# Hybrid decoder block on one core: when the mixing product's later operands are split, and who makes two SwiGLU chunks' low parts

## The chip, the cores and the metric

The kernel runs on 1 core of one Trainium2 chip. The metric is the device time of one execution in microseconds.

## The reference

One decoder block on 512 tokens of width 1024, all in float32. What matters here is the last steps of the token mixers and the channel mixer behind them:

```python
y_a = u @ conv_w_out + conv_b_out                    # 1024 x 1024
y_b = (hb * gelu(z_rg)) @ lru_w_out                  # 1280 x 1024
m = sigmoid(z_ga) * y_a + sigmoid(z_gb) * y_b
x = x + m @ w_mix_out                                # the mixing product, 1024 x 1024
h = rmsnorm(x, norm2_g)
x = x + (silu(h @ ffn_w1) * (h @ ffn_w3)) @ ffn_w2   # SwiGLU, width 2816
return rmsnorm(x, norm_f_g)
```

Ahead of these stand an input norm, one wide input projection (`w_in`), a 31-tap causal convolution with a layer norm, and a gated linear recurrence with block-diagonal gates.

## The kernel before, in words

**Matmuls in two parts.** TensorE works on the type fp32r. To keep float32 accuracy each operand is split into a high part (a cast to fp32r, made by ScalarE, `split_to`, line 133) and a low part (the operand minus its high part, a subtraction, line 129). A product is then three matmuls: high by high, high by low, low by high. The low part's engine is an argument: VectorE (`vec`) or GpSimd (`pool_e`).

**Weights.** Weights come in chunks of 128 x 1024. The list `chunks` holds them in the order of use. `emit_chunk` loads a chunk into one of 4 raw buffers (`raws`) through the SP queue, casts its high part on ScalarE and subtracts its low part on the engine that the chunk names (`lo`), into one of 5 buffers (`hls`). `weights(key, ahead)` first emits all chunks up to `ahead` (4 as a rule) behind the one asked for. Tiles `hl_mxb` and `hl_mxt` are chunks of `w_mix_out`, `hl_fb` and `hl_ft` those of the SwiGLU weights.

**The mixing product.** `m @ w_mix_out` and the last SwiGLU product are made by the class `Sevenfold`, with seven products of half size where eight would be plain. Inner blocks are numbered k = 0 to 3. `tile` and `pair` make, on VectorE, sums and differences of the quarters of `m` for each k; `ops[k]` holds a pair that is split at once (`u_`, `sp`) and two tiles that are not split yet, `e` and `va`. `run` makes the products:

- The first pass goes over k = 0 to 3 with the operands `u_` and `sp` into three pairs of PSUM banks, r1, r2 and r5. In the last k the two row blocks of r1 and r2 end first, and `plus` (line 1000, its addition at line 940) adds each into `x2`, the residual stream: four additions of 128 x 512 on VectorE.
- `split_late` splits `e` and `va` of one k, into `mxeb` and `mxvb`: two casts on ScalarE and two subtractions on VectorE. It is called after each k of the first pass once k is at least `lag`, and after each k of the second pass until all are split. `lag` is 0 for the mixing product (`m7`) and `LATE_LAG`, 8, for the last product (`o7`).
- The second pass (`second`) goes over k = 0 to 3 with `e` and `va` into banks r7, r1 and r3; r1 goes on accumulating, so it waits for the additions that read it, and r3 takes the banks of r2. Behind the first k of it four additions take r5 into `x2`.
- The last k and the rest (`third`) stand in `mix_end`, with six more additions, the second norm's statistics, the scaled rows `xs` and their transposes `th` (line 579).

`mix_end` also loads weights for sums that GpSimd makes for later products (`piece_sums`, tiles `fws` and `fwso`, lines 129 and 394), and `full` adds high and low parts on GpSimd (line 1078).

**The order of work.** Most engines' instructions are put in order by the framework: of those that are ready in its own planning, the one traced first is issued first. `tc.manual_schedule` keeps the traced order for the engines it names; it is used for the end of the mixing product but not for its two passes. `tc.issue_after(ins)` queues what is traced inside it, on the engine of `ins`, behind `ins`; instructions on other engines are not bound by it.

**The two SwiGLU chunks.** Blocks 1 and 2 of the SwiGLU product (`BEGUN`) begin early. Their first chunks, `fb11_1`, `fb21_1`, `fb11_2`, `fb21_2`, follow the chunks of `w_mix_out` in the list, and the reach ahead emits the first three of them during the second pass of the mixing product. The list is made by these lines:

```python
for k in BEGUN:
    f_both("b11", k)
    f_both("b21", k)
```

Of the kernel before, what the change touches and what calls it, by code (L numbers as in the profile page):

```python
# [52 lines left out]
BEGUN, BEGUN_LATER = (1, 2), (3,)  # L53
# [1 line left out]
SUMS_DENSE, SUMS_OWN, SUMS_EACH = 20, 52, (60, 68)  # L55


F_MIX, OUT_MIX, LATE_LAG = 2, 1, 8
OUT_IN = 1

KEPT = {2: 1, 3: 2, 4: 3, 5: 4, 6: 5, 7: 6, 8: 7, 9: 7, 10: 7}
# [35 lines left out]
def tile_block(ctx, tc, a, out):  # L97
# [19 lines left out]
    def bank(name):  # L117
        return psum.tile([P, T], F32, tag="mm", name=name)

    def bank2(name):  # L120
        return psum2.tile([P, T], F32, tag="cv", name=name)

    vec, act, pe, pool_e = nc.vector, nc.scalar, nc.tensor, nc.gpsimd
# [15 lines left out]
    def split(name, full, eng, p_=None, copy=act.copy):  # L139
        p_ = p_ or pairt(name)  # L140
        return split_to(*p_, full, eng, copy)
# [7 lines left out]
    def wchunk(key, src, kt, cols, where="hl", lo=pool_e, after=None):  # L149
        chunks.append((key, src, kt, cols, where, lo, after))  # L150
# [101 lines left out]
    class Quartered:  # L252
        def __init__(self, name, w, kh, lo, parts=(), step=None):


            self.name, self.w, self.kh = name, w, kh
            self.step = step or 1
            self.tile = lambda k, i: k + kh * i if self.step == 1 else 2 * k + i
            self.parts = {n: [None] * kh for n in parts}

            self.all_sums = [dram.tile([P, 4, T], F32, tag=f"{name}t_{k}", name=f"{name}t_{k}") for k in range(kh)]
            self.sums = {(n, k): self.all_sums[k][:, i, :] for i, n in enumerate(IN_PLACE) if n not in parts for k in range(kh)}
            self.at = {}

            def quarter(n, k):
                if n[0] == "t":
                    return self.sums[n, k]
                i, h = int(n[1]) - 1, int(n[2]) - 1
                return w[:, self.tile(k, i), h * T : (h + 1) * T]

            def chunk(key, of):
                def load(raw_t):
                    for i, q in enumerate(of):
                        nc.sync.dma_start(raw_t[:, i * T : (i + 1) * T], quarter(*q))

                for i, q in enumerate(of):
                    self.at[q] = (f"{name}{key}", i)
                wchunk(f"{name}{key}", load, len(of), T, lo=lo)


            for p_ in (("b11", "t1", "b21"), ("t2", "t3", "b22"), ("t4",)):
                p_ = [n for n in p_ if n not in parts]
                for k in range(kh):
                    if len(p_) % 2 and k % 2 == 0:
                        chunk(f"{p_[-1]}_{k}", [(p_[-1], i) for i in (k, k + 1) if i < kh])
                    if len(p_) > 1:
                        chunk(f"{p_[0]}_{k}", [(n, k) for n in p_[:2]])
# [4 lines left out]
        def get(self, k, *names, ahead=AHEAD):  # L292

            out = []
            for n in names:
                if n in self.parts:
                    out.append(self.parts[n][k])
                    continue
                key, i = self.at[n, k]
                if key not in self.loaded:  # L300
                    self.loaded[key] = weights(key, ahead)
                h, l = self.loaded[key]
                out.append((h[:, i, :], l[:, i, :]))
            return out
# [22 lines left out]
    mixq = Quartered("mx", a["w_mix_out"][0].rearrange("(k p) n -> p k n", p=P), ND // 2, vec, ("t1", "t4"))  # L327
# [7 lines left out]
    def f_quarter(n, k, w_, c0, c1):  # L335

        c, j = 4 * (int(n[1]) - 1), 2 * k + int(n[2]) - 1
        return w_[:, c + c0 : c + c1, j * P : (j + 1) * P]
# [7 lines left out]
    def f_both(n, k, lo=vec):  # L346

        def load(raw_t):
            for i, w_ in enumerate((w1, w3)):
                if n[0] == "b":  # L350
                    src = f_quarter(n, k, w_, 0, 4)
                else:
                    c, e, _ = WHERE[n]
                    src = f_sums[k][:, i, int(c[1]), :].rearrange("p (k n) -> p k n", k=4)[:, :, e * P : (e + 1) * P]
                newest["any"] = nc.sync.dma_start(raw_t[:, i * T : (i + 1) * T].rearrange("p (k n) -> p k n", k=4), src).ins

        wchunk(f"f{n}_{k}", load, 8, P, lo=lo)
# [81 lines left out]
            yield  # L439

    for k in BEGUN:
        f_both("b11", k)
        f_both("b21", k)

    for k in BEGUN:
        f_both("t4", k, vec if k == BEGUN[0] else pool_e)
# [340 lines left out]
    behind = [None, None]  # L787
# [160 lines left out]


    class Sevenfold:  # L950
        def __init__(self, q, lag=0):
            self.lag, self.kept = lag, 0
            self.q, self.uv, self.ops, self.waiting = q, [], [], []
            self.name, self.kh = q.name, q.kh

# [37 lines left out]
        def run(self, sums, begun, end):  # L993

            n, kh, get = self.name, self.kh, self.q.get
            quarter = lambda p_, cs: tuple(v[:, cs] for v in p_)
            plus = lambda t, h, b_: add(sums[t][h], b_, sums[t][h])  # L1000
            late = []

            def split_late():
                k = len(late)
                if k < kh:
                    late.append((split(f"{n}eb{k}", self.ops[k][2], vec), split(f"{n}vb{k}", self.ops[k][3], vec)))

            r1, r2 = ([bank(f"{n}{r}{i}") for i in range(2)] for r in ("r1", "r2"))
            r5 = [bank2(f"{n}r5{i}") for i in range(2)]
            for k in range(kh):  # L1010
                wb21, wb11, wt1 = get(k, "b21", "b11", "t1")
                u_, sp, e, va = self.ops[k]
                todo = [(r1, quarter(u_, LO), wb11), (r2, quarter(u_, HI), wb21), (r5, (sp[:, LO], sp[:, HI]), wt1)]
                ends = k == kh - 1
                order = [(r, i) for i in range(2) for r in (0, 1)] + [(2, 0), (2, 1)] if ends else [(r, i) for r in range(3) for i in range(2)]
                for r, i in order:
                    self.product(todo[r][0], i, *todo[r][1:], k == 0, ends)
                    if ends and r == 1:
                        plus(i, 0, r1[i])
                        plus(i, 0, r2[i])  # L1020
                if k >= self.lag:
                    split_late()
                begun(k)
            r7, r2 = ([bank(f"{n}{r}{i}") for i in range(2)] for r in ("r7", "r3"))

            def second(k, wb22, wt2, wt3):
                e, va = late[k]
                todo = [(r7, quarter(e, HI), wt3), (r1, quarter(va, LO), wt2), (r2, quarter(e, LO), wb22)]
                ends = k == kh - 1
                order = [(r, i) for i in range(2) for r in (1, 2)] + [(0, 0), (0, 1)] if ends else [(r, i) for r in range(3) for i in range(2)]  # L1030
                for r, i in order:
                    self.product(todo[r][0], i, *todo[r][1:], r != 1 and k == 0, ends, r == 1)

            def third(i, ks):
                for k in ks:
                    self.product(r1, i, quarter(late[k][1], HI), *get(k, "t4"), False, k == kh - 1, True)

            for k in range(kh - 1):
                second(k, *get(k, "b22", "t2", "t3"))
                split_late()  # L1040
                if k == 0:
                    for i in range(2):
                        plus(i, 1, r5[i])
                        plus(2 + i, 1, r5[i])

            act.activation(warm, late[-1][1][0][:, :1].bitcast(F32), AF.Sqrt, scale=0.0, bias=eps_t)
            last = get(kh - 1, "b22", "t2", "t3", ahead=AHEAD - 1)
            end(lambda: second(kh - 1, *last), plus, r1, r2, r7, third)

    m7 = Sevenfold(mixq)  # L1050
    for n, j in enumerate(mixq.order()):
        ws = w_tiles(f"co{j}", ND)
        ps = bank(f"ya{j}")
# [410 lines left out]
```

## Time and profile before

| what | value |
|---|---|
| median of 3 runs | 798.24 us (798.44, 798.24, 797.44) |
| span of the profiled execution | 797.3 us |
| TensorE busy | 786.5 us (99%) |
| VectorE busy | 696.8 us (87%) |
| ScalarE busy | 473.2 us (59%) |
| GpSimd busy | 359.9 us (45%) |
| mean granted TensorE clock | 0.997 |

The page gives the profiled execution's span, from its first to its last instruction, and no other time of that execution; the median of the runs is 0.94 us over that span. Engines are named PE (TensorE), PEld (its weight loads), DVE (VectorE), ACT (ScalarE), POOL (GpSimd) and SP (SyncE, which issues most DMAs). A row of a timeline has start and duration in us, engine, line, operation, what is written from what, and in brackets the idle time before it with what ended that. A row of the table of windows has the stretch, its length, the busy time of PE, PEld, DVE, ACT and POOL with the number of instructions, the granted clock, the DMA share and GB/s. A line such as L129 or L940 is that of a helper which many parts use, so the tile names tell the instructions apart.

### The profile page before, as it was taken

Reading aid. Unit: us, or ns where it says so; the run is one execution under the profiler, and the core shown is the slowest. Engines: PE = TensorE matmul, PEld = TensorE weight load, DVE = VectorE, ACT = ScalarE, POOL = GpSimd, SP = SyncE. Lnnn points to the kernel's source line nnn. Section 1 sums busy time; section 2 is a strip of 40 time slices with the busy share of each in tenths; the row PEclk is TensorE's granted clock in tenths of the full one; section 3 lists DMA queues with packets and bytes.
Section 4 is the critical chain, followed back from the end, with each engine's and each line's share of the span. In section 5 each row is a group of like instructions: output and inputs, shape, how many; then the busy total and the mean of one; then the engine's idle time right before and its main releaser. Section 6 shows DMA issues by size and latency. Waiting matters only on the chain.

```text
span 797.3 us, 12582 instructions
## 1 busy us (share of the span) xinstructions
PE 786.5 (99%) x4374; PEld 689.1 (86%) x4374; DVE 696.8 (87%) x1097; ACT 473.2 (59%) x674; POOL 359.9 (45%) x347
## 2 busy tenths in 40 slices
PE   8999999999999999999999999999999999999996
PEld 7988888888888888888887898999999999888885
DVE  5899999999998997985799968898877798999956
ACT  7546688777679654562326467554555555556743
POOL 2576778788779988853360482113312221000000
PEclk9999999999999999999999999999999999999998
DMA  7745566577776786879887887588988898778652
GB/s 216 196 127 175 162 190 195 179 238 229 200 247 202 243 272 212 281 232 296 266 309 238 277 263 230 150 273 264 355 298 289 301 326 294 239 236 258 206 171 105
DMA packets 181074, 188.13 MB, mean 236 GB/s; under 512 B 14119, under 2 KB 142035, under 8 KB 181011
## 3 DMA queue, kind: packets, MB, share of 16 engines
q1 hardware_dynamic: 172195, 156.66, 63.1%
q0 software_dynamic: 8672, 30.41, 11.0%
q8 instruction: 34, 0.56, 0.3%
q10 hardware_dynamic: 144, 0.26, 0.1%
q14 instruction: 29, 0.24, 0.1%
HBM read 145.48 MB, written 38.80 MB: 231 GB/s over the span
## 4 chain that ended last, share of the span: by engine, by line
PE 83%; DVE 9%; DMA 4%; issue 2%; ACT 2%; SPq 0%; DVEq 0%; ACTq 0%
PE z L539 35%; PE fr L1218 24%; PE or L991 13%; PE f L539 3%; PE g L860 3%; PE mxr L991 3%; DMA raw_lo<-in_lru_w_out_dram 1%; DMA raw_co<-in_conv_w_out_dram 1%; DMA mxws<-in_w_mix_out_dram 1%; PE fr L1262 1%; DVE hl_co L129 1%; PE yb L539 1%; DVE hl_mxb L129 1%; DVE mxws L129 1%; DVE sga L1056 1%
## 5 line engine op out<-in xcount | busy, mean ns | idle before, releaser
L733 DVE SCALAR_TENSOR_TENSOR cv<-u,par,cv 128x511 f32<-128x511 f32 (+17 forms) x240 | 162.6, 728 | 1.1 <-ACT cv L730 0.9
L129 POOL TENSOR_TENSOR hl_in<-raw_in,hl_in 128x1024 fp32r<-128x1024 f32 x51 | 123.2, 2422 | 63.6 <-ACT hl_in L133 45.1
L129 POOL TENSOR_TENSOR fws<-fws 128x256 f32<-128x256 f32 x120 | 104.6, 874 | 78.6 <-DMA fws<-in_ffn_w_dram 72.9
L398 POOL DMA_DIRECT2D ot<-fwso x21 | 15.3, 731 | 164.4 <-DVE fwso L129 156.7
L1218 PE MATMUL fr<-hs_0h,hl_ft 128*128 128x256 f32 x320 | 59.2, 283 | 0.0
L133 ACT CAST hl_in<-raw_in 128x1024 fp32r<-128x1024 f32 x51 | 53.2, 1043 | 3.2 <-POOL fws L394 1.3
L129 DVE TENSOR_TENSOR hl_ft<-raw_ft,hl_ft 128x1024 fp32r<-128x1024 f32 x39 | 47.5, 1218 | 5.5 <-ACT hl_ft L133 5.5
L1218 PEld LDWEIGHTS fr<-hs_0h,hl_ft 128*128 128x128 f32 x320 | 50.6, 192 | 0.0
L133 ACT CAST hl_ft<-raw_ft 128x1024 fp32r<-128x1024 f32 x40 | 41.8, 1046 | 13.2 <-PE fr L1218 9.9
L129 DVE TENSOR_TENSOR hl_fb<-raw_fb,hl_fb 128x1024 fp32r<-128x1024 f32 x30 | 36.7, 1222 | 14.6 <-ACT hl_fb L133 13.8
L1218 PE MATMUL fr<-hs_0l,hl_ft 128*128 128x256 f32 x160 | 45.3, 283 | 0.0
L133 ACT CAST hl_fb<-raw_fb 128x1024 fp32r<-128x1024 f32 x30 | 31.5, 1050 | 20.8 <-PE fr L1218 13.3
L539 PE MATMUL z<-h10h,hl_in 128*128 128x512 f32 (+1 forms) x110 | 41.4, 378 | 0.0
L539 PE MATMUL z<-h17h,hl_in 128*128 128x512 f32 (+1 forms) x110 | 41.1, 376 | 0.0
L539 PE MATMUL z<-h11h,hl_in 128*128 128x512 f32 (+1 forms) x110 | 41.1, 376 | 0.0
L539 PE MATMUL z<-h13h,hl_in 128*128 128x512 f32 (+1 forms) x110 | 41.1, 376 | 0.0
L539 PE MATMUL z<-h14h,hl_in 128*128 128x512 f32 (+1 forms) x110 | 41.1, 376 | 0.0
L539 PE MATMUL z<-h15h,hl_in 128*128 128x512 f32 (+1 forms) x110 | 41.1, 376 | 0.0
L539 PE MATMUL z<-h16h,hl_in 128*128 128x512 f32 (+1 forms) x110 | 41.1, 376 | 0.0
L539 PE MATMUL z<-h12h,hl_in 128*128 128x512 f32 (+1 forms) x110 | 41.1, 375 | 0.0
L133 ACT CAST hl_ob<-raw_ob 128x1024 fp32r<-128x1024 f32 (+1 forms) x23 | 23.4, 1016 | 23.4 <-PE or L991 10.5
L394 POOL TENSOR_TENSOR fws<-fws 128x256 f32<-128x256 f32 x40 | 31.6, 792 | 2.8
(962 smaller groups left out, 2640.6 us busy)
## 6 DMA issues: line engine op xcount, KB each, us to landing
raw_in<-in_w_in_dram SPq DMA_DIRECT2D x52, 512.0 KB
fws<-in_ffn_w_dram SPq DMA_DIRECT2D x80, 256.0 KB
raw_ft<-fs SPq DMA_DIRECT2D x34, 512.0 KB
fs<-fws SPq DMA_DIRECT2D x23, 512.0 KB
ot<-fwso POOLq DMA_DIRECT2D x21, 512.0 KB, 6.0
fwso<-in_ffn_w_dram POOLq DMA_DIRECT2D x40, 256.0 KB, 7.1
fs<-fws POOLq DMA_DIRECT2D x17, 512.0 KB, 4.9
raw_ob<-in_ffn_w_dram SPq DMA_DIRECT2D x33, 256.0 KB
```

Source lines behind the costliest of these rows:

```text
L129: return eng.tensor_tensor(out=o, in0=x, in1=y, op=ALU.subtract)
L133: copy(h, full)
L394: eng.tensor_tensor(out=q11, in0=q22, in1=q11, op=ALU.add)
L398: return queue.dma_start(dest, raw.rearrange("p (m n) -> p m n", m=dest.shape[1]))
L539: pe.matmul(ps, l, r, start=i == 0, stop=i == n - 1)
L733: vec.scalar_tensor_tensor(out=acc[c][:, s:], in0=u[c][:, : T - s], scalar=dw(c, s), in1=acc[c][:, s:], op0=ALU.mult, op1=ALU.add)
L860: pe.matmul(ps, l, r, start=k == 0, stop=k == len(mms) - 1)
L991: pe.matmul(banks[i], l_[:, ts], r_, start=start and n == 0, stop=stop and n == 2, skip_group_check=again)
L1056: vec.scalar_tensor_tensor(out=o, in0=ps, scalar=pc("conv_b_out", j), in1=o, op0=ALU.add, op1=ALU.mult)
L1218: pe.matmul(ps[:, HALVES[i]], lw[:, c, :], rx_, start=not (again or i or c or m), stop=bool(i and c == 3 and m == 2), skip_group_check=True,)
L1262: pe.matmul(self.r4[:, HALVES[i]], lw, rx_, start=not (i or c or m), stop=bool(i and c == 3 and m == 2), skip_group_check=True)
```

## The change

Three things change. `MIX_LATE_LAG` is 2, so in the first pass of the mixing product `split_late` is called after k = 2 and after k = 3 instead of after each k; the parts of k = 2 and 3 are traced after the first and the second k of the second pass. A new flag `behind`, set for the mixing product, puts the `split_late` after the last k of the first pass under `tc.issue_after` of the last of the four additions. And the low parts of the chunks `fb11_1` and `fb21_1` are made by GpSimd instead of VectorE.

```diff
-F_MIX, OUT_MIX, LATE_LAG = 2, 1, 8
+F_MIX, OUT_MIX, MIX_LATE_LAG, LATE_LAG = 2, 1, 2, 8
...
     for k in BEGUN:
-        f_both("b11", k)
-        f_both("b21", k)
+        for n in ("b11", "b21"):
+            f_both(n, k, pool_e if k == BEGUN[0] else vec)
...
     class Sevenfold:
-        def __init__(self, q, lag=0):
-            self.lag, self.kept = lag, 0
+        def __init__(self, q, lag=0, behind=False):
+            self.lag, self.kept, self.behind = lag, 0, behind
...
-            late = []
+            late, last_sum = [], None
...
                     if ends and r == 1:
                         plus(i, 0, r1[i])
-                        plus(i, 0, r2[i])
+                        last_sum = plus(i, 0, r2[i]).ins
                 if k >= self.lag:
-                    split_late()
+                    with tc.issue_after(last_sum) if last_sum and self.behind else nullcontext():
+                        split_late()
                 begun(k)
...
-    m7 = Sevenfold(mixq)
+    m7 = Sevenfold(mixq, MIX_LATE_LAG, True)
```

## The prediction

> **What bounds the kernel now.** I read the page first: one engine fills the span.
>
> ```profile
> span 797.3 us, 12582 instructions
> PE 786.5 (99%) x4374; PEld 689.1 (86%) x4374; DVE 696.8 (87%) x1097; ACT 473.2 (59%) x674; POOL 359.9 (45%) x347
> ```
>
> TensorE is busy in all but 10.8 us of 797.3. Next I cut the span into three stretches with the table of windows, leaving out the start (to 12 us) and the tail (from 787 us), which the change does not touch.
>
> ```profile
> 12.00:434.00 422.00, 422.00 (x1955) 353.24 (x1955) 385.25 (x578) 263.44 (x348) 287.87 (x251) 1.00 0.72 220
> 434.00:440.00 6.00, 4.62 (x20) 3.23 (x19) 6.00 (x10) 3.79 (x6) 0.00 (x0) 1.00 1.05 359
> 440.00:787.00 347.00, 346.91 (x2337) 322.05 (x2336) 294.61 (x483) 194.82 (x292) 68.95 (x90) 1.00 0.79 256
> ```
>
> The second number is TensorE's busy time. Between 12 and 787 us it idles 1.38 us in the one stretch 434 to 440 and 0.09 us in all the rest. So this kernel offers one hole, and it is the turn from the first pass to the second of the mixing product. The timeline of TensorE shows the hole, and the blocks behind it give the undisturbed pace.
>
> ```profile
> 434.70 0.61 PE L991 MATMUL mxr<-hl_mxt,mxeb0h 128*128 128x512 f32 x2
> 436.72 0.40 PE L991 MATMUL mxr<-hl_mxt,mxvb0l 128*128 128x512 f32 x1
> 438.50 0.73 PE L991 MATMUL mxr<-hl_mxt,mxvb0h 128*128 128x512 f32 x2 [1.38 <-DVE x L940]
> 440.67 0.62 PE L991 MATMUL mxr<-hl_mxt,mxeb1h 128*128 128x512 f32 x2
> 444.75 0.62 PE L991 MATMUL mxr<-hl_mxt,mxeb2h 128*128 128x512 f32 x2
> 448.83 0.62 PE L991 MATMUL mxr<-hl_mxt,mxvb3h 128*128 128x512 f32 x2
> 449.28 0.39 PE L991 MATMUL mxr<-hl_mxt,mxvb3l 128*128 128x512 f32 x1
> ```
>
> Blocks 1 and 2 of the second pass (18 matmuls each) take 444.75 - 440.67 = 4.08 and 448.83 - 444.75 = 4.08 us, 0.227 a matmul. Block 0 takes 440.67 - 434.70 = 5.97. It loses 1.89 us: the wait named on the 438.50 row and slower restarts around it. The releaser is a VectorE addition at L940, `plus`, which takes a first-pass bank into `x2`; block 0 accumulates on into that bank, so it must wait. VectorE's timeline says why the addition is late.
>
> ```profile
> 434.75 0.69 DVE L129 TENSOR_TENSOR mxeb1l<-mxe,mxeb1h 128x512 fp32r<-128x512 f32 x1
> 435.36 0.68 DVE L940 TENSOR_TENSOR x<-mxr,x 128x512 f32<-128x512 f32 x1
> 435.95 0.68 DVE L129 TENSOR_TENSOR mxvb1l<-mxv,mxvb1h 128x512 fp32r<-128x512 f32 x1
> 436.56 0.68 DVE L940 TENSOR_TENSOR x<-mxr,x 128x512 f32<-128x512 f32 x1
> 437.15 0.68 DVE L129 TENSOR_TENSOR mxeb2l<-mxe,mxeb2h 128x512 fp32r<-128x512 f32 x1
> 437.75 0.68 DVE L940 TENSOR_TENSOR x<-mxr,x 128x512 f32<-128x512 f32 x1
> ```
>
> Additions and low parts alternate, 0.60 us apart. The third addition (bank r1 of row block 1) ends at 437.75 + 0.68 = 438.43, and TensorE restarts at 438.50. The low parts of k = 1 and 2 between them are not needed until 440.67 and 444.75.
>
> **The later parts.** With `MIX_LATE_LAG` 2 the parts of k = 0 are made in the first pass after k = 2, those of k = 1 after k = 3 with their VectorE half queued behind the fourth addition, those of k = 2 and 3 in the second pass. Per k this moves two casts on ScalarE and two subtractions on VectorE, and no DMA. Three low parts leave the places ahead of the third addition (the 434.75, 435.95 and 437.15 rows): 3 x 0.60 = 1.80 us. It then ends at about 436.63. TensorE without the hole wants it three matmuls after 436.06 (six matmuls of 0.227 after 434.70), so at 436.74: the wait and the slow restarts go, 1.89 us, with at most 0.15 left since the two times nearly touch. The operands `x2` were loaded before (no addition waits on a DMA in these rows); an addition 1.8 us earlier could meet such a wait, which no row excludes, and its bound is the hole itself.
>
> What is late next? First the parts that were put back. VectorE does the same list of work, so the list ends no sooner, and the parts of k = 3 come last in it.
>
> ```profile
> 441.29 0.69 DVE L129 TENSOR_TENSOR mxvb3l<-mxv,mxvb3h 128x512 fp32r<-128x512 f32 x1
> 443.09 1.22 DVE L129 TENSOR_TENSOR hl_mxt<-raw_mxt,hl_mxt 128x1024 fp32r<-128x1024 f32 x1
> 444.22 1.28 DVE L940 TENSOR_TENSOR x<-mxr,x 128x512 f32<-128x512 f32 x2
> 445.42 1.22 DVE L129 TENSOR_TENSOR hl_fb<-raw_fb,hl_fb 128x1024 fp32r<-128x1024 f32 x1
> 446.62 1.22 DVE L129 TENSOR_TENSOR hl_fb<-raw_fb,hl_fb 128x1024 fp32r<-128x1024 f32 x1
> 448.75 1.25 DVE L129 TENSOR_TENSOR hl_fb<-raw_fb,hl_fb 128x1024 fp32r<-128x1024 f32 x1 [0.86 <-ACT hl_fb L133]
> 449.93 4.06 DVE L940 TENSOR_TENSOR x<-mxr,x 128x512 f32<-128x512 f32 x6
> ```
>
> The mixing work ends at 444.22 + 1.28 = 445.50. In the changed order the four additions of r5 and the last t2 chunk are traced ahead of the parts of k = 3, so I take these as last: `mxvb3l` ready near 445.5 instead of 441.98. TensorE, 1.89 earlier, wants it at 449.28 - 1.89 = 447.39. Left alone, 1.9 us of slack hides it. The casts cost nothing either, as long as ScalarE keeps the hole that its row shows:
>
> ```profile
> 440.05 1.05 ACT L133 CAST hl_mxt<-raw_mxt 128x1024 fp32r<-128x1024 f32 x1 [2.22 <-DMA raw_mxt<-mxt]
> 442.15 0.19 ACT L555 ACTIVATION_READ_ACCUMULATOR xs<-x 128x1 f32 x1
> 443.58 1.06 ACT L133 CAST hl_fb<-raw_fb 128x1024 fp32r<-128x1024 f32 x1 [1.25 <-PE mxr L991]
> 444.94 1.06 ACT L133 CAST hl_fb<-raw_fb 128x1024 fp32r<-128x1024 f32 x1 [0.30 <-PE mxr L991]
> 447.67 1.06 ACT L133 CAST hl_fb<-raw_fb 128x1024 fp32r<-128x1024 f32 x1 [1.66 <-PE mxr L991]
> ```
>
> The four casts for k = 2 and 3 are half as wide as the 1.06 us cast, an estimate of 2.1 us for all; 2.22 us are free ahead of 440.05. If that cover is gone they push the first `hl_fb` cast by up to 2 us, and nothing needs that chunk before 460.
>
> **The two low parts on GpSimd.** VectorE loses the 445.42 and 446.62 rows, 2 x 1.2 = 2.4 us. GpSimd gains two subtractions of the same form, ahead of work that waits for a DMA:
>
> ```profile
> 448.19 2.42 POOL L129 TENSOR_TENSOR fws<-fws 128x256 f32<-128x256 f32 x2 [31.50 <-DMA fws<-in_ffn_w_dram]
> 457.24 0.74 POOL L1078 TENSOR_TENSOR hf<-h20h,h20l 128x256 f32<-128x256 f32 x1 [1.77 <-DVE h20l L583]
> L129 POOL TENSOR_TENSOR hl_in<-raw_in,hl_in 128x1024 fp32r<-128x1024 f32 x51 | 123.2, 2422 | 63.6 <-ACT hl_in L133 45.1
> 460.26 0.28 PE L1218 MATMUL fr<-h20h,hl_fb 128*128 128x256 f32 x1
> ```
>
> One takes 2.42 us by the group of its form. The casts ahead of them wait on TensorE, so they come 1.89 earlier: the first can start at 441.69, behind the two squares at 442.34, and GpSimd starts at about 442.8 to 443.4 and ends the second at 447.6 to 448.2. The chunk is first used at 460.26 - 1.89 = 458.4, which is 10 us later. The queue behind them, the SwiGLU weights' sums, is held until 448.2 at most, where its DMA lets it begin at 448.19 now; if that DMA comes 1.9 earlier too, the sums lose up to 1.9 us of it and end no later than now, and the 1.77 us that GpSimd idles at 457.24 is cover besides.
>
> The price is elsewhere. Two rows from a much earlier stage show what a VectorE subtraction with both inputs in SBUF does while such a GpSimd subtraction runs:
>
> ```profile
> 171.13 2.40 POOL L129 TENSOR_TENSOR hl_in<-raw_in,hl_in 128x1024 fp32r<-128x1024 f32 x1
> 171.53 2.54 DVE L129 TENSOR_TENSOR xb7l<-xb,xb7h 128x512 fp32r<-128x512 f32 x1
> ```
>
> The VectorE one starts 0.40 after GpSimd's, ends 0.54 after GpSimd's end (174.07 against 173.53), and takes 2.54 instead of 0.69: it stood until GpSimd was done. The additions do not: six at 449.93 take 4.06 us, 0.68 each, while GpSimd makes the sums that begin with the 448.19 row; they read one input from PSUM. The Trainium skill, GPSIMD Engine Reference, section 8 "Key points", says that GpSimd shares its SBUF interfaces with VectorE and contends with VectorE instructions that have two SBUF inputs; these rows agree. The page gives no duration: if contention were only a slowing shared by both engines, the sum below would lie between -1.79 and its own -0.94; by the row, in which VectorE stands still, it is -0.94.
>
> So which VectorE work falls into 443 to 448? The third `hl_fb` (the 448.75 row) stays on VectorE; its cast ends at 447.67 + 1.06 - 1.89 = 446.84. If GpSimd holds until 447.6 or 448.2, it ends 1.2 later at 448.8 to 449.4. Behind it on VectorE are the six additions of the 449.93 row, which should start at 449.93 - 1.89 = 448.04 for the full gain. They are 0.7 to 1.3 late. These feed the norm, whose scaled rows feed the transposes, without slack:
>
> ```profile
> 454.97 1.57 DVE L1098 TENSOR_SCALAR xs<-x,stats 128x512 f32<-128x512 f32 x3
> 455.63 1.15 PE L579 MATMUL th<-ident,xs 128*128 128x128 f32 x8
> 458.01 1.03 PE L579 MATMUL th<-ident,xs 128*128 128x128 f32 x8
> ```
>
> The first eight transposes take 1.15 against 1.03 for the next: they already meet the scaling rows at the moment these are made. So what the additions lose, TensorE loses. The ends are 0 (GpSimd's parts are queued behind the sums that wait for a DMA, or meet no one) and 1.3; I take 0.85, between, nearer the overlap that the casts' times give. **The sum:** -1.89 + 0.1 + 0.85 = -0.94 us. The page lists the span, 797.3; the runs' median is 798.24, 0.94 above it, and I carry the difference to the median: 797.3 us. Its own range is -1.9 to -0.3: 796.3 to 797.9.
>
> **The rivals.** *The last parts meet GpSimd.* If `mxeb3l` and `mxvb3l` are still undone when GpSimd starts at about 443, they stand behind it. One 2.42 us subtraction ahead of `mxvb3l` makes it ready at 445.5 + 2.4 = 447.9, a wait of 0.5; two make it 450.3, a wait of 2.9. In both cases the third `hl_fb` part comes after both: 450.3 + 1.2 = 451.5, and the additions start 451.5 - 449.93 = 1.6 later than now. With no slack at the transposes that is +1.5 us: 799.7, and 800.5 if one more GpSimd operation of the 457.24 row's 0.74 slips between. It decides from the point where GpSimd starts before about 444.3, when two parts of 0.6 are still to do. For it: VectorE's list ends at 445.5. Against it: those parts are ready early and the order could put them ahead of the r5 additions, which end 2.4 us sooner or later by that. This is the slower side.
>
> *The parts are not out of the way.* Only the parts of k = 1 are queued behind the additions; those of k = 2 and 3 are merely traced later, and any that is ready while an addition is not goes first. Two of them between cost 1.2 of the 1.89: with the GpSimd part then half hidden, 797.9.
>
> *The order changes elsewhere.* Everything after is placed by readiness, and TensorE has no hole to absorb a new wait; 800 to 801 as an open end, on no row.
>
> **How the numbers follow.** Forecast 0.50, the last parts meet GpSimd 0.31, parts not out of the way 0.10, the order elsewhere 0.09. About 0.2% (1.6 us) is what a measurement of this kernel tells from no change. Faster by more than that needs 796.6, the best two fifths of the forecast case: 0.21. Slower by more needs 799.84: two thirds of the first rival and most of the last, 0.28. The rest, 0.51, is within. The range takes the forecast, the second rival and most of the first: 796.3 to 800.3; about 0.04 lies below and 0.14 above.
>
> **What would show it.** Right: the idle time on the first `mxr` matmuls of the second pass is gone and the four additions stand together on VectorE from about 434.8. The lows of `hl_fb` appear on POOL from about 443; the VectorE `hl_fb` at 447 takes 1.8 or more, and TensorE has a wait of 0.7 to 1.3 at `th`. If that wait is absent the gain is the full 1.8. If instead an `mxr` matmul waits on `mxvb3l` near 447.4, the first rival holds. A wait of `mxr` on L940 that remains says that the parts still stand between. A wait after 465 would say that I have missed the place altogether.

## The result and the profile after

The changed kernel takes 801.62 us (median of 4 runs, 800.99 to 802.75); the kernel before, beside it on the same chip, 797.88 us. The ratio is 1.0044 [1.0031, 1.0056]: slower by about 3.5 us, and outside the range of 796.3 to 800.3. A second set of 12 runs gave 802.64 us against 798.33, ratio 1.0041 [1.0024, 1.0057]. (Ratios leave out disturbed runs, so they can differ a little from the quotient of the medians.) The profiled execution of after took 800.99 us, 1.89 over its span.

The table of windows of after, over the stretches of the prediction:

```profile
434.00:440.00 6.00, 6.00 (x28) 4.99 (x27) 5.79 (x10) 2.20 (x4) 0.00 (x0) 1.00 1.07 363
440.00:787.00 347.00, 344.76 (x2322) 318.80 (x2321) 293.87 (x479) 196.68 (x297) 74.87 (x92) 1.00 0.80 256
```

The hole at the turn is closed (6.00 of 6.00 us busy, 4.62 before). But behind 440 TensorE now idles 2.24 us where it idled 0.09. TensorE's timeline of after shows where:

```profile
434.87 0.62 PE L991 MATMUL mxr<-hl_mxt,mxeb0h 128*128 128x512 f32 x2
453.27 0.50 PE L991 MATMUL mxr<-mxt40h,mxvb0h 128*128 128x512 f32 x1 [0.32 <-DVE x L940]
454.77 0.27 PE L579 MATMUL th<-ident,xs 128*128 128x128 f32 x1
455.43 0.98 PE L579 MATMUL th<-ident,xs 128*128 128x128 f32 x7 [0.40 <-DVE xs L1099]
459.22 1.61 PE L579 MATMUL th<-ident,xs 128*128 128x128 f32 x8 [1.43 <-DVE h20l L583]
462.06 0.28 PE L1219 MATMUL fr<-h20h,hl_fb 128*128 128x256 f32 x1
```

The last row is the first SwiGLU matmul. Read the row of 459.22 with care: these transposes wait for `h20l`, which frees the bank that they write. VectorE's timeline of after says what `h20l` stood behind, and GpSimd's what held that:

```profile
433.60 2.87 DVE L940 TENSOR_TENSOR x<-mxr,x 128x512 f32<-128x512 f32 x4
447.59 1.23 DVE L129 TENSOR_TENSOR hl_fb<-raw_fb,hl_fb 128x1024 fp32r<-128x1024 f32 x1 [0.79 <-ACT hl_fb L133]
448.80 0.68 DVE L940 TENSOR_TENSOR x<-mxr,x 128x512 f32<-128x512 f32 x1
449.94 3.28 DVE L940 TENSOR_TENSOR x<-mxr,x 128x512 f32<-128x512 f32 x5 [0.46 <-DVE x L940]
453.32 1.19 DVE L1099 TENSOR_SCALAR xs<-x,stats 128x512 f32<-128x512 f32 x1
454.61 4.16 DVE L1099 TENSOR_SCALAR xs<-x,stats 128x512 f32<-128x512 f32 x3
458.69 0.47 DVE L583 SCALAR_TENSOR_TENSOR h20l<-th,par,h20h 128x256 fp32r<-128x256 f32 x1
```

```profile
447.69 2.54 POOL L129 TENSOR_TENSOR fws<-fws 128x256 f32<-128x256 f32 x2 [32.17 <-DMA fws<-in_ffn_w_dram]
451.83 2.39 POOL L129 TENSOR_TENSOR hl_fb<-raw_fb,hl_fb 128x1024 fp32r<-128x1024 f32 x1
454.18 1.78 POOL L129 TENSOR_TENSOR fws<-fws 128x256 f32<-128x256 f32 x2
455.93 2.55 POOL L129 TENSOR_TENSOR hl_fb<-raw_fb,hl_fb 128x1024 fp32r<-128x1024 f32 x1
```

**First cost: scalings held by GpSimd.** The four additions stand together as planned. GpSimd's low parts came behind the first sums, which wait 32.17 us for their DMA, and so fell on the norm's four scalings `xs`: three of them take 4.16 us where the same row took 1.57 before. A scaling that meets the low part of 455.93 starts at 456.17 and ends at 458.77, after 2.60 us; before, it took 0.47. The kernel before shows a small hold too, on its first scaling beside GpSimd's shorter sums (VectorE's timeline of before):

```profile
454.10 0.77 DVE L1098 TENSOR_SCALAR xs<-x,stats 128x512 f32<-128x512 f32 x1
```

**Second cost: a late table load.** ScalarE's timeline of after shows why the six additions start at 448.80, 13.93 us after the start of the second pass, and not 13.31 us after it as in the executions without a wait below (e8, e11):

```profile
439.64 1.05 ACT L133 CAST hl_mxt<-raw_mxt 128x1024 fp32r<-128x1024 f32 x1 [3.80 <-DMA raw_mxt<-mxt]
442.83 0.61 ACT L133 CAST mxvb3h<-mxv 128x512 fp32r<-128x512 f32 x1
444.42 1.28 ACT L1047 ACT_TABLE_LOAD   x1
445.71 0.29 ACT L1047 ACTIVATE warm<-mxvb3h,eps_t 128x1 f32<-128x1 f32 x1
445.91 0.61 ACT L555 ACTIVATE xs<-x 128x512 f32<-128x512 f32 x1
446.52 1.04 ACT L133 CAST hl_fb<-raw_fb 128x1024 fp32r<-128x1024 f32 x1
```

`warm` is a dummy activation at the end of `run`; it is there to load the square root's table ahead of the norm, and it reads the high part of the last k, `mxvb3h`. With the parts of k = 3 made last, the table load moved with them, from 1.5 us after the first matmul of the second pass to 444.42 - 434.87 = 9.55 us after it. Load, `warm` and square now stand in front of the third `hl_fb` cast, while ScalarE sits idle for 3.80 us ahead of 439.64.

### The profile page after: what moved, and what is told of

The parts are those of the page before. It is cut to its first block, busy times and chain, and to the rows that moved or that the text cites. A ratio compares the mean times of both kernels' runs of the same rounds, so it can differ in the third digit from the quotient of the medians.

```text
span 799.1 us, 12584 instructions
## 1 busy us (share of the span) xinstructions
PE 786.8 (98%) x4374; PEld 688.4 (86%) x4374; DVE 696.8 (87%) x1095; ACT 472.2 (59%) x674; POOL 366.4 (46%) x349
## 4 chain that ended last, share of the span: by engine, by line
PE 95%; DVE 2%; ACT 1%; DMA 1%; issue 0%; SPq 0%; DVEq 0%
PE z L539 35%; PE fr L1219 24%; PE or L991 13%; PE yb L539 7%; PE ya L539 5%; PE mxr L991 3%; PE f L539 3%; PE g L860 3%; PE fr L1263 1%; DVE xs L1099 1%; DMA x<-in_x_dram 1%; DVE x L940 0%; PE z L632 0%; PE th L579 0%; ACT hl_fb L133 0%
## 5 line engine op out<-in xcount | busy, mean ns | idle before, releaser
L129 DVE TENSOR_TENSOR hl_fb<-raw_fb,hl_fb 128x1024 fp32r<-128x1024 f32 x28 | 34.3, 1224 | 13.9 <-ACT hl_fb L133 13.9
L133 ACT CAST hl_ob<-raw_ob 128x1024 fp32r<-128x1024 f32 (+1 forms) x23 | 23.3, 1014 | 24.2 <-PE or L991 12.7
```

The lines of the kernel that those rows point to most:

```text
L129: return eng.tensor_tensor(out=o, in0=x, in1=y, op=ALU.subtract)
L133: copy(h, full)
```

## The experiments

Two theories at first: the loss is GpSimd's low parts (A), or the later parts and the order that follows from them (B). The first four kernels share a chip; before there: 798.49 us.

**e1: the later parts alone.** Both low parts back on VectorE:

```diff
-            f_both(n, k, pool_e if k == BEGUN[0] else vec)
+            f_both(n, k, vec)
```

> The changed kernel with both SwiGLU chunks' low parts back on VectorE. All times against the kernel before. Theory A (the later parts close the 1.9 us hole; the loss comes from GpSimd's two subtractions, which hold VectorE's four scaling operations xs ahead of the transposes): no hole at 436 to 438, xs operations of 0.5 to 0.8 us, no wait of 1.4 us at th; two low parts of 1.2 us stand on VectorE ahead of the norm again, so the gain is between 0.8 and 1.9 us. Rival B (the later parts themselves make the loss, by casts and low parts that come too late): the kernel stays 1.5 to 4 us slower.

799.21 us, ratio 1.0015 [1.0001, 1.0028]. Most of the loss is gone, so GpSimd carries most of it; but nothing is gained, and the time lies in neither theory's range. In the profiled execution (own time 800.26) the additions of the turn came late in spite of the change, 436.12 to 438.99, and TensorE waited twice for them (idle 0.76 and 0.36), then 0.51 and 0.32 for the six additions. The four scalings took 0.47 to 0.78, as in before: no long hold.

**e2: GpSimd's low parts alone**, in the order of before:

```diff
-        f_both("b11", k)
-        f_both("b21", k)
+        for n in ("b11", "b21"):
+            f_both(n, k, pool_e if k == BEGUN[0] else vec)
```

> The kernel before with only the two chunks' low parts on GpSimd. Theory A: the hole at 436 to 438 stays and the xs operations are held, so the loss is larger than the changed kernel's by up to the 1.9 us of the hole: 3 to 6 us slower than before. Rival B: within 1 us of before.

798.48 us, ratio 1.0007 [0.9982, 1.0031]: no loss, as B had it. So A alone falls. GpSimd's timeline of this kernel shows where the low parts came to lie:

```profile
443.60 2.40 POOL L129 TENSOR_TENSOR hl_fb<-raw_fb,hl_fb 128x1024 fp32r<-128x1024 f32 x1 [27.38 <-ACT hl_fb L133]
447.12 2.42 POOL L129 TENSOR_TENSOR fws<-fws 128x256 f32<-128x256 f32 x2 [1.12 <-DMA fws<-in_ffn_w_dram]
449.50 2.41 POOL L129 TENSOR_TENSOR hl_fb<-raw_fb,hl_fb 128x1024 fp32r<-128x1024 f32 x1
```

One is ahead of the sums, the other beside the six additions, which read PSUM and took their 4.06 us. The same two instructions cost nothing or two microseconds by their place in GpSimd's queue, and the later parts moved that place.

**e3: the low parts first.** The changed kernel, with the sums queued behind them:

```diff
-                piece_sums(*made[-1], pool_e)
+                with tc.issue_after(newest["sub"]):
+                    piece_sums(*made[-1], pool_e)
```

> The changed kernel with GpSimd's sums of the SwiGLU weights queued behind its two low parts, so that GpSimd makes the low parts at 443 to 448 instead of behind the sums' DMA wait. Theory A: the xs operations are no longer held by subtractions of 2.4 us; instead VectorE's last parts mxeb3l and mxvb3l and the third hl_fb low part meet them (the prediction's first rival): a wait of 0.5 to 1.5 us at an mxr matmul near 447 and additions up to 1.6 us late, in all between 1 us faster and 2 us slower than before, and faster than the changed kernel. If the place of the low parts does not matter (rival: GpSimd is simply slower and its later work is late) the time stays that of the changed kernel, 3.7 us slower.

799.8 us, ratio 1.0025 [1.0015, 1.0035]. This is the place that the prediction had assumed, and in it the first rival's mechanism appears (GpSimd, VectorE and TensorE timelines, one fence each):

```profile
442.90 5.21 POOL L129 TENSOR_TENSOR hl_fb<-raw_fb,hl_fb 128x1024 fp32r<-128x1024 f32 x2 [27.77 <-ACT hl_fb L133]
```

```profile
443.31 2.53 DVE L129 TENSOR_TENSOR mxeb3l<-mxe,mxeb3h 128x512 fp32r<-128x512 f32 x1
445.77 2.88 DVE L129 TENSOR_TENSOR mxvb3l<-mxv,mxvb3h 128x512 fp32r<-128x512 f32 x1
```

```profile
448.71 0.50 PE L991 MATMUL mxr<-hl_mxt,mxvb3l 128*128 128x512 f32 x1 [1.10 <-DVE stats L556]
```

The last parts stand behind GpSimd, 2.53 and 2.88 instead of 0.68, and a matmul waits for `mxvb3l` (the row names the small operation behind it; `mxvb3l` ends at 445.77 + 2.88 = 448.65). The scalings are unheld (1.28 for three). One hold is traded for another.

**e4: the scalings on ScalarE.** The changed kernel, with the first half's four `xs` made by activations:

```diff
+            if t < 2:
+                act.activation(sc[t][i], x2[t][i], AF.Copy, scale=r)
+                return
...
-            rs = [scaled(t, 1, (0,)) for t in range(2)]
-            for t in range(2):
-                scale(t, 1, rs[t])
+            rs = [scaled(t, 1, ()) for t in range(2)]
+            for i in range(2):
+                for t in range(2):
+                    scale(t, i, rs[t])
```

The edit also changes the order of the four among themselves.

> The changed kernel with the first four scaling operations xs (row blocks 0 and 1) made by ScalarE instead of VectorE; nothing else moves. Theory A: ScalarE's operations are not held while GpSimd subtracts: each takes about 0.6 us, the wait of 1.4 us at th goes, and the time is 1.5 to 4 us less than the changed kernel's, near before or up to 1 us faster. Rival C (the loss is in the stores and loads that wait for GpSimd's sums, or spread elsewhere): the time stays within 0.8 us of the changed kernel's.

799.25 us, ratio 1.0019 [1.0005, 1.0033]: by the ratios about 1.8 to 2.0 us less than the changed kernel, with GpSimd's low parts still behind the first sums. That fits the held scalings, by size and place; e14 against e12 below shows it row by row. The profiled execution was one of its longer ones (802.72) and shows a third place, from TensorE's, VectorE's and GpSimd's timelines:

```profile
475.61 0.83 PE L579 MATMUL th<-ident,xs 128*128 128x128 f32 x4 [1.66 <-DVE h24l L583]
```

```profile
471.75 3.41 DVE L129 TENSOR_TENSOR hl_ft<-raw_ft,hl_ft 128x1024 fp32r<-128x1024 f32 x1
```

```profile
471.50 2.57 POOL L129 TENSOR_TENSOR hl_ft<-raw_ft,hl_ft 128x1024 fp32r<-128x1024 f32 x1
```

GpSimd, late by its two extra subtractions, starts its `hl_ft` part a quarter microsecond ahead of VectorE's; that takes 3.41, and `h24l` behind it 1.66 of TensorE's time.

**e7: the changed kernel again**, nothing edited.

> The changed kernel once more, nothing edited, for a second profile and a narrower interval. Theory (the two GpSimd low parts fall behind the sums that wait for a DMA, onto VectorE's four scalings xs, and the six additions start late): slower than before by 2.5 to 4 us, and the profile again shows GpSimd's two hl_fb low parts after the first sums, at 451 to 458, one or more xs scalings of over 1.5 us beside them, and waits at th of 2 us or more in sum. Rival (the profiled execution was an odd one, and the time comes from the later parts alone): the hl_fb low parts lie elsewhere or the scalings take 0.47 to 0.8 each, and the loss is the same.

802.64 us, ratio 1.0041 [1.0024, 1.0057]. TensorE and VectorE, in a second execution:

```profile
460.04 1.68 PE L579 MATMUL th<-ident,xs 128*128 128x128 f32 x8 [1.41 <-DVE h20l L583]
```

```profile
455.43 4.16 DVE L1099 TENSOR_SCALAR xs<-x,stats 128x512 f32<-128x512 f32 x3
```

The hold is the same to a few hundredths. It belongs to the order, not to the execution. The waits at `th`, 0.29 and 1.41, come to 1.70 us, a little less than the 2 that were expected.

**e8: the kernel before again**, one execution with a profile.

> The kernel before, nothing edited, for a profile of another execution. Theory (the hole at the turn of the passes depends on how far VectorE lies behind TensorE, which differs between executions): the idle time of TensorE between 434 and 440 lies anywhere from 0.2 to 2 us, and is small if the first low part of the mixing chunk behind it starts over 2 us ahead of the second pass. Rival (the hole is a fixed 1.9 us of this order): 1.4 idle and 1.9 lost again, with the same rows.

797.94 us, span 796.0. The table of windows and TensorE's timeline:

```profile
434.00:440.00 6.00, 6.00 (x28) 4.99 (x27) 6.00 (x10) 5.33 (x8) 0.00 (x0) 1.00 1.12 353
```

```profile
435.35 0.62 PE L991 MATMUL mxr<-hl_mxt,mxeb0h 128*128 128x512 f32 x2
439.43 0.62 PE L991 MATMUL mxr<-hl_mxt,mxeb1h 128*128 128x512 f32 x2
454.40 1.12 PE L579 MATMUL th<-ident,xs 128*128 128x128 f32 x8
459.02 0.28 PE L1218 MATMUL fr<-h20h,hl_fb 128*128 128x256 f32 x1
```

Block 0 takes 439.43 - 435.35 = 4.08 us, as the others do: with the very same code the hole isn't there. From the first of these matmuls to the end of the span are 796.0 - 435.35 = 360.65 us; in the profiled execution of the prediction they were 797.3 - 434.70 = 362.60. The hole of 1.89 is all but 0.06 of the difference. What differs is how far VectorE lies behind TensorE at the turn, as its timeline of e8 shows:

```profile
432.50 0.68 DVE L129 TENSOR_TENSOR mxeb1l<-mxe,mxeb1h 128x512 fp32r<-128x512 f32 x1
```

This is 2.85 us ahead of the second pass; in the execution of the prediction the same operation starts at 434.75, 0.05 behind it. Which of VectorE's earlier waits sets that was not settled.

**e9 and e10: the low parts on VectorE, but queued later**, the first behind the four scalings, the second behind `h20l` to `h23l`; e9 on the changed order, e10 on that of before. The edit is the same in both:

```diff
+            if lo is None:
+                act.copy(h, rv)
+                deferred.append(lambda: sub(vec, l, rv, h.bitcast(F32)))
...
+            deferred.pop(0)()
```

> The changed kernel with the two low parts back on VectorE but queued later there: the first behind the four xs scalings, the second behind the four h20l to h23l. Nothing of them stands ahead of the six additions or beside the scalings. Theory (loss from scalings held by GpSimd and from late additions; the later parts by themselves gain what the hole is in that execution): 0.5 to 1.5 us faster than before, about 797.0 to 798.0 on the scale of 798.5, no wait at 436 to 438, th waits under 1 us in sum. Rival (the later parts themselves cost, by an order that changes further on): 799 or more, as with the later parts alone, and waits that stand elsewhere.

> The kernel before (parts early, as before) with the same two low parts queued later on VectorE as in the run before this. Theory: the six additions start up to 2 us earlier against the second pass, the hole at the turn stays: 0 to 1 us faster than before, and 0.3 to 1.5 us slower than the changed order with the same queueing. Rival (the later parts cost rather than gain): this one is the faster of the two by 0.5 us or more.

e9: 799.49 us, ratio 1.0015 [1.0, 1.003]; e10: 799.1 us, 1.002 [0.9998, 1.0042]. Both missed what was expected; e9 lies where its rival put it. The queueing has a price of its own: `h24l` now stands behind a low part, and the first SwiGLU matmul comes 24.96 us after the start of the second pass in e10, 23.67 in e8 (0.32 of this is a small hole at the turn in e10). And e9, with no GpSimd part and no hole, still waits for the six additions (TensorE's timeline of e9):

```profile
452.05 0.50 PE L996 MATMUL mxr<-mxt40h,mxvb0h 128*128 128x512 f32 x1 [0.36 <-DVE x L945]
454.04 0.50 PE L996 MATMUL mxr<-mxt40h,mxvb0h 128*128 128x512 f32 x1 [0.32 <-DVE x L945]
```

In e9, as in after, e7 and e3, the table load comes 9.54 to 9.55 us after the start of the second pass and the third `hl_fb` cast 11.65 us after it; in e8, e2 and e10, at 1.51 to 1.52 and 11.08 to 11.40. That made the table load the suspect for what the later parts cost.

**e11 and e12: the table load early.** `warm` reads the high part of k = 1; e11 is e1 with that edit, e12 the changed kernel with it:

```diff
-            act.activation(warm, late[-1][1][0][:, :1].bitcast(F32), ...)
+            act.activation(warm, late[1 if kh == 4 else -1][1][0][:, :1].bitcast(F32), ...)
```

> The later parts alone (both hl_fb low parts on VectorE), with the small warming activation of ScalarE reading the high part of k = 1 instead of that of k = 3, so that the table load is not carried behind the last part. Theory (the later parts carry ScalarE's table load from 1.5 us after the start of the second pass to 9.5 us, it pushes the third hl_fb cast from 11.1 to 11.65, and the six additions and the transposes follow): the load lies at 2 to 5 us after that start, the third hl_fb cast at 11.1, the first of the six additions at 12.2 to 12.7, the th wait under 0.3 us; 0.5 to 1.2 us faster than the later parts alone (799.2), so 797.9 to 798.7, same as before or a little faster. Rival (the later parts cost by VectorE's list, which is full anyway): the load is early and the additions still start at 13.9 or later, 799 or more.

> The changed kernel with only that warming activation reading the high part of k = 1. Theory (two costs side by side: the table load about 0.85 us, the scalings xs held by GpSimd 2 to 3 us): the six additions 0.5 to 1.5 us earlier against the second pass, the scalings still held (one or two of 1.5 to 2.6 us), 0.3 to 1.2 us faster than the changed kernel: 800.5 to 801.8, still slower than before. Rival (the hold is all, and takes up what the additions gain, since GpSimd's low parts stay where the DMA puts them): no change, 801.5 to 802.6.

e11: 798.07 us against 798.56, ratio 0.9987 [0.9972, 1.0002]. Windows, ScalarE and VectorE of e11:

```profile
434.00:440.00 6.00, 6.00 (x29) 4.95 (x28) 5.90 (x9) 4.32 (x7) 0.00 (x0) 1.00 1.12 357
440.00:465.00 25.00, 25.00 (x145) 21.85 (x144) 23.20 (x41) 14.01 (x32) 16.12 (x20) 1.00 0.89 272
```

```profile
435.23 1.28 ACT L1047 ACT_TABLE_LOAD   x1
445.84 1.06 ACT L133 CAST hl_fb<-raw_fb 128x1024 fp32r<-128x1024 f32 x1 [0.32 <-PE mxr L991]
```

```profile
448.07 4.07 DVE L940 TENSOR_TENSOR x<-mxr,x 128x512 f32<-128x512 f32 x6
```

The load is in the idle time, the third cast waits only for TensorE, the six additions run together, and TensorE has no wait at all from 434 to 465. The second pass starts at 434.76, so 795.4 - 434.76 = 360.64 us are left to the end: the 360.65 of e8. In this execution nothing is left of what the later parts cost. The six additions start 13.31 us after the second pass, not at the 12.2 to 12.7 that was expected, and that is early enough. Against e1, though, the table load is not all that differs. In e1's profiled execution VectorE is late from the turn on, and its third `hl_fb` low part starts without a wait for its cast (VectorE's timeline of e1):

```profile
449.52 1.69 DVE L129 TENSOR_TENSOR hl_fb<-raw_fb,hl_fb 128x1024 fp32r<-128x1024 f32 x1
```

So that trace does not show the table load as what e1 lost. The changed kernel with and without the edit is the cleaner pair. e12: 800.12 us, ratio 1.0021 [1.0005, 1.0038], by the ratios about 1.6 to 1.8 us less than the changed kernel, where 0.3 to 1.2 were expected. The held scalings stay, as TensorE's timeline of e12 shows:

```profile
453.87 0.27 PE L579 MATMUL th<-ident,xs 128*128 128x128 f32 x1
454.60 0.98 PE L579 MATMUL th<-ident,xs 128*128 128x128 f32 x7 [0.46 <-DVE xs L1099]
458.38 1.61 PE L579 MATMUL th<-ident,xs 128*128 128x128 f32 x8 [1.42 <-DVE h20l L583]
461.22 0.28 PE L1219 MATMUL fr<-h20h,hl_fb 128*128 128x256 f32 x1
```

These rows give each cost its size. Count from the start of the second pass (434.87 in after, 434.60 in e12, 435.35 in e8):

| us after the start of the second pass | after | e12 | e8 |
|---|---|---|---|
| first transpose | 19.90 | 19.27 | 19.05 |
| first SwiGLU matmul | 27.19 | 26.62 | 23.67 |
| between the two | 7.29 | 7.35 | 4.62 |

After loses 27.19 - 23.67 = 3.52 us. Of this 0.6 goes with the late table load and 0.2 remains ahead of the transposes without it; 2.7, most of it, is lost at the transposes, where the scalings are held. The times credit e12 with more than these 0.6; what the rest is, no row shows.

**e14: both mended.** e4 with the early table load.

> The changed kernel with both mended: the warming activation reads the high part of k = 1, and the four scalings xs are made by ScalarE. The two low parts stay on GpSimd. Theory (the two costs together are the whole loss): 798.0 to 798.9, within 0.2% of before, with waits of TensorE at th under 0.6 us in sum. Rival (a third cost that neither explains): 799.3 or more as with the scalings alone on ScalarE.

799.93 us, ratio 1.0026 [1.0005, 1.0047]: missed, and in the rival's range. The profiled execution (798.0) has no wait over 0.12 us at `th`, and 796.2 - 434.66 = 361.54 us to the end. Between the first transpose (453.94) and the first SwiGLU matmul (459.11) lie 5.17 us, where e12 has 7.35 and e8 4.62: in these executions, taking the scalings off VectorE gives back 2.2 us of the 2.7. But 4 of its 12 runs took 802.4 to 805.5. The `hl_ft` collision that e4's longer execution showed can explain these; none of them was profiled, so that is argued, not shown. Such long runs also occur without low parts on GpSimd (e10: 805.16 and 805.01).

**e15: e11 once more.**

> The later parts alone with the early table load once more, for a narrower interval on the version that came out best. Theory (no wait is left at the turn or at th, so it gains what the hole of the kernel before costs on a mean execution): 0.2 to 0.8 us faster than before, ratio about 0.9993, and no wait of over 0.3 us between 434 and 465. Rival (the first result was chance): ratio 1.000 to 1.002.

799.03 us against 798.51, ratio 1.0007 [0.9988, 1.0027]. The profile has no wait here either (797.2 - 436.50 = 360.70 us to the end); its second pass only starts 1.7 us later than in e11, and that is lost ahead of the second pass. The time lies in the rival's range: e11's lead was not confirmed. So the version that came out best cannot be told from the kernel before; no gain over it is shown. Nor do the times alone tell e15 (1.0007) from e1 (1.0015); that the early load takes the wait away rests on the profiles.

## Why the prediction was wrong, by its steps

- **The hole and its closing: the mechanism held, the size failed.** In both profiled executions of the changed kernel the additions stand together and the hole is gone. But 1.89 us was read from one execution. The runs take 1.7 to 2.2 us over their spans, so its own time is an estimated 799.2 (797.3 + 1.9) and not 798.24: longer than any of the listed runs, and the hole is enough to explain that. e2 lost 0.29 and e8 nothing at the same place. The step "I carry the difference to the median" hid it. Nor did the later parts always close the hole (e1, e4).
- **"The casts cost nothing ... 2.22 us are free" failed.** The free time is there (3.80 in after), but three of the four casts came after it, and what hung on the last of them was not counted: `warm`, which reads it, and its table load of 1.28 us. The prediction did not follow the readers of a moved part. The claim that nothing needs the `hl_fb` chunk before 460 left out the third of these chunks, though the prediction names it further on: its low part stands ahead of the six additions on VectorE, and the cast's 0.57 us delay (11.65 against 11.08 us after the start of the second pass) went straight to them. e12 shows it by taking it away: the cast is back at 11.08 and the first addition at 13.31. This is the smaller of the two costs, 0.6 us.
- **GpSimd's place failed.** It was taken from the time at which the casts end, ahead of the sums (443 to 448); the order put both parts behind the first sums and their DMA. The sum even named that case and priced it at 0, as meeting no one; it measured 2.7 us. The sign that the prediction gave for its own mechanism did not come either: VectorE's `hl_fb` at 447.59 took 1.23 us, not 1.8 or more. A wait at `th` did come, but from the scalings.
- **Who can be held failed.** Only VectorE operations with two inputs in SBUF were looked for. The scalings have one, and were held up to 2.60 us; before already had a scaling of 0.77 at 454.10 beside GpSimd's sums, against 0.47 for the last two. The prediction quoted the Trainium skill, GPSIMD Engine Reference, section 8, for operations with two SBUF inputs; the same sentence also names a two-port mode of VectorE. The Trainium skill, SBUF — State Buffer, "Who interferes with whom", counts `tensor_scalar` among the operations that can enter it if their operands meet its conditions, and says that whoever issues first keeps the ports for its whole instruction. The rows agree: the scaling ends at 458.77, 0.29 us behind GpSimd's operation (455.93 + 2.55 = 458.48).
- **"No slack at the transposes" held.** TensorE loses 0.32 for late additions and 0.40 and 1.43 for late scalings, with no cover.
- **The first rival** had the right kind of loss at the wrong place. e3, which puts GpSimd where it assumed, measured 799.8 where it said 799.7, with the wait at `mxvb3l`. That the two times meet is in part luck: e3 also carries the late table load, which the rival did not have. In the changed kernel itself "the order changes elsewhere" came true, to which the prediction gave 0.09.
- **The six additions** have one more term that stays open: in after the second starts 0.46 after the first has ended, in e11 only 0.10. The same 0.45 to 0.46 stands in e3, e4, e7, e9, e12 and e14, so with the later parts wherever the two low parts are not on VectorE ahead of the additions; the row names the addition before it in after and TensorE in e12. It is the likely place of the 0.2 us that e12 still lacks ahead of the transposes.

## What to carry to other kernels

Before moving work later, list everything that reads it, dummy instructions too: an activation that only warms a table takes the table load along. Before moving work to GpSimd, fix its place in the queue and look at every VectorE operation beside that place, those with one SBUF input as well; the same subtraction cost nothing beside additions from PSUM and two microseconds beside scalings. And read a hole in a second execution before pricing it: this one was 1.89 us in one and absent in the next.

## What the runs showed of the hardware

- A VectorE operation between SBUF operands that starts during a GpSimd subtraction stood still until that ended, in these rows: `mxvb3l` took 2.88 for 0.68 us, `xs` 2.60 for 0.47, `hl_ft` 3.41 for 1.22; additions that read PSUM kept 0.68.
- A table load took 1.28 us and `warm` began 0.01 after it (444.42 + 1.28 = 445.70, 445.71): no further pause beside it.
- The start of the second pass lay between 434.38 and 436.50 us in the 14 profiled executions, changes or none; from there to the end, e8, e11 and e15, which have no wait at the turn or at `th`, agree within 0.06 us (360.65, 360.64, 360.70). Of a change of this size, that stretch tells more than the span.
